# Attention's values as two products of reduced-width parts, with the weights scaled on ScalarE

## The chip, the cores and the metric

The kernel runs on one core of one Trainium2 chip. The metric is the device time of one execution in microseconds (us), the median of several runs. Engines are called PE (TensorE; PEld is its weight load), DVE (VectorE), ACT (ScalarE), POOL (GpSimd) and SP (SyncE, which issues the DMAs).

## What is computed

A two-layer trunk for 1024 prompt tokens and 64 sample tokens. Each layer projects the normalised input once, feeds three branches (a gated linear recurrence, a sparse attention, a state-space scan), and projects their concatenation back. The change touches the end of the attention branch:

```python
logits = jnp.einsum('bqgrd,bqkgd->bqgrk', qg, ksel) * (ATT_HEAD_DIM ** -0.5)
logits = jnp.where(valid, logits + bias, -jnp.inf)
p = jax.nn.softmax(logits, axis=-1)
o = jnp.einsum('bqgrk,bqkgd->bqgrd', p, vsel)
y_b = o * jax.nn.silu(ga)
```

There are 8 query heads in 2 groups (`g`) of 4, head size 64. The kernel keeps all keys and masks those that are not selected.

## The kernel before

Products with full precision are mostly made of float32r parts: a matrix is split into a high part (a float32r copy) and a low part (the rest), and the products of the parts are summed in PSUM. `three` (L210) does this for the projections: L215, L216 and L217 are its three products. Attention's logits (L1068) use two parts. The values (L1098) do not: they multiply plain float32 operands.

Attention works on items `(t, g)`: a tile `t` of 128 queries (t = 8 is the 64 sample tokens) and a head group. The list `todo` gives their order: all of g = 0, the wide ones (t = 5, 8, 7, 6) last, then g = 1 as t = 2, 1, 0, 3, 8, 4, 5, 6, 7. A tile t has 128(t+1) keys; t = 8 has 576. For each item

- `queries` loads and splits the queries, and transposes them (L1034);
- `weigh` makes for each of the 4 heads the logits in PSUM (L1068), adds mask and bias and takes the maximum on DVE (L1071), exponentiates on ACT (L1075), and scales the row by the reciprocal of its sum on DVE (L1077, L1078);
- `values` goes over blocks of 128 keys. For each block PE transposes the weights of the 4 heads into one of two `tp` banks (L1093), ACT copies that bank to SBUF as `pT` (L1095), and PE multiplies with the values (L1098), the stationary operand being 64 columns of `vt`, one matmul for each pair of heads, into the two halves of the partitions of the single `s1` bank. At the end DVE multiplies with the gate (L1100) and DMAs store the result.

There are 82 blocks in each layer: 72 with 128 queries, 10 of the sample tile with 64. Two items are in flight: `weigh` of the next item is written ahead of `values` of this one, and the weights live in 8 buffers `lg`.

The order on each engine is not that of the source. A scheduler that simulates the program while it is built places each instruction by priority, as soon as its own model of the engines has it ready. So attention, which comes first in the source, is interleaved on PE with the first half of the output projection that follows it (`out_proj(0, ...)`: 576 products of L215 to L217). These products are called the filler here: they depend on the other branches only, and PE takes them where the scheduler saw attention waiting.

The values `vt` come from three DMAs at the start of attention (L980 to L982), beside the loads of the keys (L986 to L989), which pass through two of the `lg` buffers.

Of the kernel before, what the change touches and what calls it, by code (L numbers as in the profile page):

```python
# [10 lines left out]
F32 = mybir.dt.float32  # L11
F32R = mybir.dt.float32r
# [25 lines left out]
TS = 64  # L38
# [44 lines left out]
def body(ctx, tc, I, O):  # L83
# [36 lines left out]
    def s1_bank():  # L120
        return bank("s1", 1)
# [157 lines left out]
    for l in range(DEPTH):  # L279
# [684 lines left out]
                    done(d, ci, a, b, ps)  # L964

        kst = kp.tile([128, 2, 2, TP + PAST + TS], F32R, name="kst")
        vt = kp.tile([128, 13, 128], F32, name="vt")
        def near_bias(g):

            nb = kp.tile([128, 4, 256], F32, name="nb")  # L970
# [6 lines left out]

        nb = near_bias(0)

        SP.dma_start(vt[:, 0:8, :], kvd[:, 0:8, 128:256])  # L980
        SP.dma_start(vt[:, 8:12, :], I["cache_att_v"][l])
        SP.dma_start(vt[:TS, 12, :], kvd[:TS, 8, 128:256])  # L982
        kf, kc_ = [p.tile([128, 1024], F32, name="lg", bufs=8) for _ in range(2)]
        kf = kf.rearrange("p (t c) -> p t c", c=128)
        SP.dma_start(kf, kvd[:, 0:8, 0:128])
# [52 lines left out]
        def weigh(t, g, qst):  # L1038

            nq = rows_of(t)  # L1040
            kbase, nk, near, nb0 = reach(t)
            far = nk - near
            mk = mask[t - 2] if t >= 2 else None

            parts = [(c, min(c + 512, far), False) for c in range(0, far, 512)]
            if parts and parts[-1][1] - parts[-1][0] + near <= 512:
                banks = [[x] for x in parts[:-1]] + [[parts[-1], (far, nk, True)]]
            else:
                banks = [[x] for x in parts] + [[(far, nk, True)]]
            mx = p.tile([128, 4, 4], F32, name="mx")  # L1050
            sm = p.tile([128, 4], F32, name="sm")
            ri = p.tile([128, 4], F32, name="ri")
            lgs = []
            for h in range(4):
                lg = p.tile([128, 1024], F32, name="lg", bufs=8)
                lgs.append(lg)
                k_ = 0
                if mk is not None:
                    nbm = p.tile([128, 256], F32, name="nbm")
                    G.tensor_tensor(nbm[:nq, :near], nb[:nq, h, nb0:nb0 + near], mk[:nq, far:nk], op=OP.add)  # L1060
                    nbm = nbm[:nq, :near]
                else:
                    nbm = nb[:nq, h, nb0:nb0 + near]
                for bank_ in banks:
                    a, b = bank_[0][0], bank_[-1][1]
                    ps = s2_bank()
                    for pt in range(2):
                        PE.matmul(ps[:nq, :b - a], qst[:, h, :nq], kst[:, g, pt, kbase + a:kbase + b],  # L1068
                                  start=pt == 0, stop=pt == 1)
                    for f, e, varies in bank_:  # L1070
                        V.tensor_tensor_reduce(lg[:nq, f:e], ps[:nq, f - a:e - a], nbm if varies else mk[:nq, f:e], 1.0,  # L1071
                                               3.0e38 if k_ == 0 else mx[:nq, h, k_ - 1:k_], OP.add, OP.min,
                                               mx[:nq, h, k_:k_ + 1])
                        k_ += 1
                S.activation(lg[:nq, :nk], lg[:nq, :nk], AF.Exp, scale=-1.0, bias=mx[:nq, h, k_ - 1:k_],  # L1075
                             accum_out=sm[:nq, h:h + 1])
                V.reciprocal(ri[:nq, h:h + 1], sm[:nq, h:h + 1])  # L1077
                V.tensor_scalar(lg[:nq, :nk], lg[:nq, :nk], ri[:nq, h:h + 1], None, op0=OP.mult)  # L1078
            return lgs

        def values(t, g, lgs):

            nq = rows_of(t)
            nk = reach(t)[1]
            ga = p.tile([128, 2, 128], F32, name="ga", bufs=1)
            SP.dma_start(ga[:, :, :nq], gad[:, 2 * g:2 * g + 2, t * 128:t * 128 + nq])
            av = s1_bank()[:, :256].rearrange("p (r q) -> p r q", r=2)
            nb_ = (nk + 127) // 128
            for j in range(nb_):
                n = min(128, nk - 128 * j)  # L1090
                ps = tp_bank()
                for i, h in enumerate((0, 2, 1, 3)):
                    PE.transpose(ps[:n, i * nq:(i + 1) * nq], lgs[h][:nq, j * 128:j * 128 + n], ident[:nq, :nq])  # L1093
                pT = p.tile([128, 4, 128], F32, name="pT")
                S.activation(pT[:n, :, :nq], ps[:n, :4 * nq].rearrange("p (r q) -> p r q", r=4), AF.Copy)  # L1095
                vj = j + (8 if t == 8 else 0)
                for b in range(2):
                    PE.matmul(av[64 * b:64 * b + 64, :, :nq], vt[:n, vj, 64 * g:64 * g + 64], pT[:n, 2 * b:2 * b + 2, :nq],  # L1098
                              start=j == 0, stop=j == nb_ - 1)
            V.scalar_tensor_tensor(ga[:, :, :nq], av[:, :, :nq], 0.5, ga[:, :, :nq], op0=OP.mult, op1=OP.mult)  # L1100
            for i in range(2):
                SP.dma_start(ybd[2 * g + i][:, t * 128:t * 128 + nq], ga[:, i, :nq])

# [130 lines left out]
```

## Time and profile before

| what | value |
|---|---|
| median of 3 runs | 2048.23 us (2042.67 to 2052.76) |
| the profiled execution's own time | 2043.88 us |
| its span | 2042.1 us |
| PE busy | 1952.6 us (96%) |
| DVE busy | 1519.2 us (74%) |
| ACT busy | 1231.8 us (60%) |
| POOL busy | 651.2 us (32%) |
| mean granted TensorE clock | 0.983 |

The span reaches from the first to the last instruction; the own time lies 1.8 us above it. The two layers do the same work, and attention stands once in each: in the first from about 700 to 948 us of the span, in the second from about 1709 to 1955 us. Busy shares over the whole span mix stages with different limits; the rows further down are cut by stage.

### The profile page before, as it was taken

What the parts mean: (1) busy time and instruction counts of PE and PEld (TensorE: products, weight loads), DVE (VectorE), ACT (ScalarE), POOL (GpSimd) and SP (SyncE); (2) the same over time, 40 slices, a digit from 0 to 9 for tenths busy, and PEclk for the clock granted to TensorE, in tenths of its full rate; (3) what the DMA queues carried; (4) which work ended last, traced back from release to release, by engine and by line L of the source; (5) the groups of instructions that cost most, each with busy time, mean ns of one, the idle gap of its engine ahead of it and who ended that gap; (6) DMA issues with size and microseconds to landing.
All of it is one profiled execution on the core that took longest, in us unless ns stands there. A gap on an engine that the chain in (4) does not pass through costs nothing.

```text
span 2042.1 us, 34620 instructions
## 1 busy us (share of the span) xinstructions
PE 1952.6 (96%) x12056; PEld 1747.9 (86%) x12056; DVE 1519.2 (74%) x3701; ACT 1231.8 (60%) x2567; POOL 651.2 (32%) x561
## 2 busy tenths in 40 slices
PE   6999999989999899999999999999899999999999
PEld 5899989888889787866998999999888887888589
DVE  7778899898866855574386888999987678566723
ACT  6569988753656544454355798987446655444621
POOL 3012244333522422253430213353245224223320
PEclk9999999999999899999999999999999998999999
DMA  6125354535332732324541343545353346234145
GB/s 228 62 72 143 101 167 123 173 105 154 107 109 83 231 116 89 106 89 137 191 134 38 108 124 108 161 137 165 99 163 97 96 149 197 90 99 140 46 145 169
DMA packets 252079, 257.94 MB, mean 126 GB/s; under 512 B 31264, under 2 KB 230304, under 8 KB 251904
## 3 DMA queue, kind: packets, MB, share of 16 engines
q1 hardware_dynamic: 251904, 255.73, 40.9%
q8 instruction: 95, 1.56, 0.3%
q14 instruction: 80, 0.66, 0.1%
HBM read 181.09 MB, written 74.57 MB: 125 GB/s over the span
## 4 chain that ended last, share of the span: by engine, by line
PE 66%; DVE 19%; DMA 6%; ACT 5%; issue 3%; SPq 1%; POOL 0%; DVEq 0%; ACTq 0%
PE mm L216 16%; PE mm L215 15%; PE mm L217 15%; PE s L1098 4%; PE tp L1093 4%; PE s L1068 3%; DVE u L855 2%; ACT junka L580 2%; PE s L881 1%; DMA cumB<-cumd 1%; PE s L514 1%; DMA eB<-cumd 1%; ACT cumB L742 1%; DMA xsc<-xsd 1%; PE s L791 1%
## 5 line engine op out<-in xcount | busy, mean ns | idle before, releaser
L193 POOL TENSOR_TENSOR wlo<-wraw,whi 128x1024 fp32r<-128x1024 f32 x80 | 195.4, 2442 | 364.0 <-ACT whi L192 360.3
L580 ACT ACTIVATE junka<-sc,cand 128x768 bf16<-128x768 f32 x248 | 239.4, 968 | 8.5 <-DVE sc L583 3.9
L192 ACT ACTIVATE whi<-wraw 128x1024 fp32r<-128x1024 f32 x130 | 137.1, 1054 | 135.3 <-PE mm L216 109.8
L1075 ACT ACTIVATE lg<-lg,mx 128x512 f32<-128x512 f32 (+8 forms) x144 | 111.2, 773 | 95.7 <-DVE mx L1071 95.3
L855 DVE SCALAR_TENSOR_TENSOR u<-raw,parh,u 128x384 f32<-128x384 f32 (+1 forms) x198 | 147.4, 751 | 11.7 <-POOL u L853 5.9
L1095 ACT ACTIVATE pT<-tp 128x512 f32<-128x512 f32 (+1 forms) x164 | 90.5, 568 | 108.1 <-PE tp L1093 103.5
L1060 POOL TENSOR_TENSOR nbm<-nb,shared 128x256 f32<-128x256 f32 (+1 forms) x112 | 81.2, 730 | 224.1 <-DVE mx L1071 201.8
L574 DVE TENSOR_SCALAR_CACHE_REDUCE junk<-sc,cand 128x384 bf16<-128x384 f32 (+4 forms) x194 | 139.9, 753 | 1.0
L1068 PE MATMUL s<-kst,qst 128*128 128x512 f32 (+4 forms) x448 | 120.8, 362 | 7.8 <-DVE mx L1071 7.3
L742 ACT ACTIVATE cumB<-cumB,ctk 128x128 f32<-128x128 f32 (+1 forms) x288 | 88.4, 384 | 54.3 <-DMA cumB<-cumd 47.7
L1093 PEld LDWEIGHTS tp<-identr,lg 128*128 128x128 f32 (+2 forms) x656 | 71.8, 140 | 45.6 <-issue 39.4
L1093 PE MATMUL tp<-identr,lg 128*128 128x128 f32 (+2 forms) x656 | 107.2, 278 | 0.5 <-DVE lg L1078 0.5
L1098 PE MATMUL s<-pT,vt 128*64 128x256 f32 (+2 forms) x656 | 104.8, 389 | 1.6 <-ACT pT L1095 1.6
L1078 DVE TENSOR_SCALAR lg<-lg,ri 128x512 f32<-128x512 f32 (+8 forms) x144 | 93.6, 651 | 3.3
L1143 DVE TENSOR_TENSOR xl<-xl,mm 128x384 f32<-128x384 f32 (+1 forms) x40 | 21.4, 540 | 94.1 <-PE mm L217 84.9
L1068 PEld LDWEIGHTS s<-kst,qst 128*128 128x128 f32 (+1 forms) x448 | 72.2, 188 | 21.9 <-DVE mx L1071 13.4
L215 PE MATMUL mm<-sth0a,whi 128*128 128x384 f32 (+1 forms) x228 | 82.9, 365 | 7.3 <-DVE xl L1143 2.0
L1071 DVE CUSTOM_DVE_ANT_0 lg<-s,shared 128x512 f32<-128x512 f32 (+4 forms) x112 | 61.8, 553 | 37.7 <-PE s L1068 31.9
L193 DVE TENSOR_TENSOR wlo<-wraw,whi 128x1024 fp32r<-128x1024 f32 x50 | 64.1, 1281 | 32.1 <-ACT whi L192 32.0
L216 PE MATMUL mm<-stl1a,whi 128*128 128x384 f32 (+1 forms) x228 | 79.6, 349 | 3.8 <-DVE stl1a L954 3.5
L216 PE MATMUL mm<-stl0a,whi 128*128 128x384 f32 (+1 forms) x228 | 79.8, 350 | 2.4 <-POOL stl0a L954 2.0
L778 POOL TENSOR_TENSOR hT<-hT,dec 128x512 f32<-128x512 f32 x28 | 35.9, 1282 | 144.3 <-DVE hT L780 137.0
(475 smaller groups left out, 6931.1 us busy)
## 6 DMA issues: line engine op xcount, KB each, us to landing
wraw<-in_w_in_dram SPq DMA_DIRECT2D x82, 512.0 KB, 3.5
wraw<-in_w_out_dram SPq DMA_DIRECT2D x48, 512.0 KB, 3.8
cumB<-cumd SPq DMA_DIRECT2D x32, 512.0 KB, 4.8
xsd<-u SPq DMA_DIRECT2D x48, 192.0 KB, 2.4
gz<-gzd SPq DMA_DIRECT2D x32, 256.0 KB, 3.6
xsc<-xsd SPq DMA_DIRECT2D x32, 256.0 KB, 3.5
eB<-cumd SPq DMA_DIRECT2D x56, 128.0 KB, 4.1
gzd<-g SPq DMA_DIRECT2D x32, 192.0 KB, 1.9
```

What stands on the lines that cost most here:

```text
L192: S.activation(hi, raw, AF.Copy)
L193: eng.tensor_tensor(lo, raw, hi.bitcast(F32), op=OP.subtract)
L215: PE.matmul(ps, hi[:, k, :], xh[ci][:, c0:], start=k == 0, stop=False)
L216: PE.matmul(ps, hi[:, k, :], xl[ci][:, c0:], start=False, stop=False)
L217: PE.matmul(ps, lo[:, k, :], xh[ci][:, c0:], start=False, stop=k == len(xs) - 1)
L574: V.tensor_scalar(junk, sc[j][:n], thr, None, op0=op, op1=OP.add, accum_out=out)
L580: S.activation(junk, sc[j][:n], AF.Sign, scale=-1.0, bias=cand, accum_out=out)
L855: V.scalar_tensor_tensor(u, raw[:, j:j + n], w[:, wbase + j * wstride:wbase + j * wstride + 1], u, op0=OP.mult, op1=OP.add)
L1068: PE.matmul(ps[:nq, :b - a], qst[:, h, :nq], kst[:, g, pt, kbase + a:kbase + b], start=pt == 0, stop=pt == 1)
L1075: S.activation(lg[:nq, :nk], lg[:nq, :nk], AF.Exp, scale=-1.0, bias=mx[:nq, h, k_ - 1:k_], accum_out=sm[:nq, h:h + 1])
L1093: PE.transpose(ps[:n, i * nq:(i + 1) * nq], lgs[h][:nq, j * 128:j * 128 + n], ident[:nq, :nq])
L1098: PE.matmul(av[64 * b:64 * b + 64, :, :nq], vt[:n, vj, 64 * g:64 * g + 64], pT[:n, 2 * b:2 * b + 2, :nq], start=j == 0, stop=j == nb_ - 1)
```

## The change

The values become float32r parts. `vhl` holds for each block of 128 keys and each group 128 columns: the high part of the 64 value columns beside their low part. The values are loaded into two `lg` buffers first; ACT makes the high part and POOL the low part. In `values`, ACT's copy of the transposed weights becomes the float32r high part `pT`; a new subtraction on DVE makes the low part `pl` from the PSUM bank and `pT`. Two matmuls over all four heads (512 columns) take the place of two float32 ones over two heads each (256 columns); the stationary operand is 128 columns wide, so the products with the high and with the low part of the values land in different partitions. At the end of an item ACT copies two quarters of the `s1` bank into `sm2`, shifted by 64 partitions, DVE adds the other two quarters, and the gate is multiplied from SBUF. In `weigh` the scaling by the reciprocal moves from DVE to ACT.

```diff
-        vt = kp.tile([128, 13, 128], F32, name="vt")
+        vhl = kp.tile([128, 13, 2, 128], F32R, name="vhl")
...
-        SP.dma_start(vt[:, 0:8, :], kvd[:, 0:8, 128:256])
-        SP.dma_start(vt[:, 8:12, :], I["cache_att_v"][l])
-        SP.dma_start(vt[:TS, 12, :], kvd[:TS, 8, 128:256])
+        v0, v1 = [p.tile([128, 1024], F32, name="lg", bufs=8) for _ in range(2)]
+        v0, v1 = [v.rearrange("p (t c) -> p t c", c=128) for v in (v0, v1)]
+        SP.dma_start(v0, kvd[:, 0:8, 128:256])
+        SP.dma_start(v1[:, 0:4, :], I["cache_att_v"][l])
+        SP.dma_start(v1[:TS, 4, :], kvd[:TS, 8, 128:256])
+        for v, n, a, b, c in ((v0, 128, 0, 8, 0), (v1, 128, 8, 12, 0), (v1, TS, 12, 13, 4)):
+            v = v[:n, c:c + b - a].rearrange("p t (g c) -> p t g c", g=2)
+            S.activation(vhl[:n, a:b, :, 0:64], v, AF.Copy)
+            G.tensor_tensor(vhl[:n, a:b, :, 64:128], v, vhl[:n, a:b, :, 0:64].bitcast(F32), op=OP.subtract)
...
-                V.tensor_scalar(lg[:nq, :nk], lg[:nq, :nk], ri[:nq, h:h + 1], None, op0=OP.mult)
+                S.activation(lg[:nq, :nk], lg[:nq, :nk], AF.Copy, scale=ri[:nq, h:h + 1])
...
-            av = s1_bank()[:, :256].rearrange("p (r q) -> p r q", r=2)
+            av = s1_bank().rearrange("p (r q) -> p r q", r=4)
...
-                pT = p.tile([128, 4, 128], F32, name="pT")
-                S.activation(pT[:n, :, :nq], ps[:n, :4 * nq].rearrange("p (r q) -> p r q", r=4), AF.Copy)
+                ps = ps[:n, :4 * nq].rearrange("p (r q) -> p r q", r=4)
+                pT = p.tile([128, 4, 128], F32R, name="pT")
+                pl = p.tile([128, 4, 128], F32R, name="pl")
+                S.activation(pT[:n, :, :nq], ps, AF.Copy)
+                V.tensor_tensor(pl[:n, :, :nq], ps, pT[:n, :, :nq].bitcast(F32), op=OP.subtract)
                 vj = j + (8 if t == 8 else 0)
-                for b in range(2):
-                    PE.matmul(av[64 * b:64 * b + 64, :, :nq], vt[:n, vj, 64 * g:64 * g + 64], pT[:n, 2 * b:2 * b + 2, :nq],
-                              start=j == 0, stop=j == nb_ - 1)
-            V.scalar_tensor_tensor(ga[:, :, :nq], av[:, :, :nq], 0.5, ga[:, :, :nq], op0=OP.mult, op1=OP.mult)
+                for k_, w in enumerate((pT, pl)):
+                    PE.matmul(av[:, :, :nq], vhl[:n, vj, g, :], w[:n, :, :nq], start=j == 0 and k_ == 0,
+                              stop=j == nb_ - 1 and k_ == 1)
+
+            sm2 = p.tile([128, 2, 128], F32, name="sm2", bufs=1)
+            S.activation(sm2[0:64, :, :nq], av[64:128, 0:2, :nq], AF.Copy)
+            S.activation(sm2[64:128, :, :nq], av[0:64, 2:4, :nq], AF.Copy)
+            for b in range(2):
+                c = slice(64 * b, 64 * b + 64)
+                V.tensor_tensor(sm2[c, :, :nq], sm2[c, :, :nq], av[c, 2 * b:2 * b + 2, :nq], op=OP.add)
+            V.scalar_tensor_tensor(ga[:, :, :nq], sm2[:, :, :nq], 0.5, ga[:, :, :nq], op0=OP.mult, op1=OP.mult)
```

The scheduler makes another order of it. In the changed file 6 lines stand above L1028 of before, so L1068 is now L1074, L1075 is L1081 and L1093 is L1099; the scaling is L1084, the copy to `pT` L1103, the subtraction L1104, the values' matmul L1107, the shifted copies L1111 and L1112.

PE, first layer, at the narrow items (2, 1), (1, 1) and (0, 1), early in the second head group. Before (`s_8808` is the result of item (2, 1), L1098 its values):

```order
L1098 MATMUL s_8808<-pT,vt 64x256 x2
L1034 MATMUL tp<-identr,qhl_8841 128x128 x4
L215 MATMUL mm<-sth6b,whi 128x320
L216 MATMUL mm<-stl6b,whi 128x320
L217 MATMUL mm<-sth6b,wlo 128x320
L215 MATMUL mm<-sth7b,whi 128x320
L216 MATMUL mm<-stl7b,whi 128x320
L217 MATMUL mm<-sth7b,wlo 128x320
L215 MATMUL mm<-sth0a,whi 128x384
L216 MATMUL mm<-stl0a,whi 128x384
```

The same place with the change (`s_8943` is the result of item (2, 1), `s_9034` of (1, 1)):

```order
L1107 MATMUL s_8943<-pT,vhl 128x512
L1107 MATMUL s_8943<-pl,vhl 128x512
L1099 MATMUL tp<-identr,lg 128x128 x8
L1074 MATMUL s_9083<-kst,qst 128x512 x2
L1074 MATMUL s_9094<-kst,qst 128x512 x2
L1074 MATMUL s_9105<-kst,qst 128x512 x2
L1074 MATMUL s_9116<-kst,qst 128x512 x2
L1107 MATMUL s_9034<-pT,vhl 128x512
L1107 MATMUL s_9034<-pl,vhl 128x512
L1107 MATMUL s_9034<-pT,vhl 128x512
```

The filler (L215 to L217) that stood between attention's products is gone from here; it has moved ahead, among the wide items of g = 0.

ACT, first layer, in the wide items at the end of g = 1, before (`lg` are weights, L1095 the copies of transposed blocks):

```order
L1095 ACTIVATE pT<-tp 128x512
L1075 ACTIVATE lg,sm<-lg,mx 128x896
L1075 ACTIVATE lg,sm<-lg,mx 128x1024
L1095 ACTIVATE pT<-tp 128x512 x2
L1075 ACTIVATE lg,sm<-lg,mx 128x1024
L953 ACTIVATE sth7a<-g_10657 128x384
L1095 ACTIVATE pT<-tp 128x512
L1075 ACTIVATE lg,sm<-lg,mx 128x1024
```

The same place with the change:

```order
L1103 ACTIVATE pT<-tp 128x512 x2
L1081 ACTIVATE lg,sm<-lg,mx 128x1024
L1111 ACTIVATE sm_9690<-s_9623 64x256
L1112 ACTIVATE sm_9690<-s_9623 64x256
L1103 ACTIVATE pT<-tp 128x512
L1084 ACTIVATE lg<-lg,ri 128x1024
L1081 ACTIVATE lg,sm<-lg,mx 128x1024
L1103 ACTIVATE pT<-tp 128x512 x2
L1081 ACTIVATE lg,sm<-lg,mx 128x1024
L1084 ACTIVATE lg<-lg,ri 128x1024 x2
```

Each exponential has got a scaling of its own width in the same queue, and each item two shifted copies; the copies that release PE's `tp` banks stand among them.

## Rows read from the trace of the kernel before

**Rows 1.** The page: its busy line and the engines of the chain that ended last.

```profile
PE 1952.6 (96%) x12056; PEld 1747.9 (86%) x12056; DVE 1519.2 (74%) x3701; ACT 1231.8 (60%) x2567; POOL 651.2 (32%) x561
...
PE 66%; DVE 19%; DMA 6%; ACT 5%; issue 3%; SPq 1%; POOL 0%; DVEq 0%; ACTq 0%
```

**Rows 2.** Windows, first layer's attention, cut where items (1,0), (6,0), (0,1), (8,1), (7,1) end.

```profile
core 0: us, PE busy (x) PEld busy (x) DVE busy (x) ACT busy (x) POOL busy (x), PEclk, DMA share, GB/s
707.29:845.12 137.83, 137.83 (x868) 110.84 (x867) 75.24 (x252) 62.24 (x126) 34.73 (x37) 1.00 0.34 104
845.12:868.09 22.97, 22.97 (x150) 18.97 (x151) 15.38 (x57) 12.51 (x33) 7.23 (x7) 1.00 0.46 139
868.09:901.86 33.77, 32.87 (x207) 25.54 (x205) 24.27 (x67) 17.20 (x40) 20.17 (x20) 1.00 0.39 120
901.86:947.71 45.85, 42.81 (x264) 23.87 (x262) 29.41 (x98) 29.92 (x55) 12.49 (x13) 1.00 0.17 51
```

**Rows 3.** Timeline of PE at three places: start us, us, engine, line, operation.

```profile
713.33 0.63 PE L1068 MATMUL s<-kst,qst 128*128 128x512 f32 x2
713.80 0.33 PE L215 MATMUL mm<-sth4a,whi 128*128 128x384 f32 x1
713.97 0.34 PE L216 MATMUL mm<-stl4a,whi 128*128 128x384 f32 x1
...
717.17 0.71 PE L1068 MATMUL s<-kst,qst 128*128 128x512 f32 x2
717.72 0.27 PE L1093 MATMUL tp<-identr,lg 128*128 128x128 f32 x1
...
909.05 0.66 PE L1093 MATMUL tp<-identr,lg 128*128 128x128 f32 x4
909.47 0.37 PE L1068 MATMUL s<-kst,qst 128*128 128x256 f32 x1
...
941.52 0.65 PE L1098 MATMUL s<-pT,vt 128*64 128x256 f32 x4
942.10 0.66 PE L1093 MATMUL tp<-identr,lg 128*128 128x128 f32 x4
942.69 0.65 PE L1098 MATMUL s<-pT,vt 128*64 128x256 f32 x4
```

**Rows 4.** Groups of ACT by form, 901.86 to 947.71 us.

```profile
L1095 ACT ACTIVATE pT<-tp 128x512 f32<-128x512 f32 x26 | 15.0, 593 | 10.2 <-PE tp L1093 9.5 <-PE s L1098 0.4 <-ACT lg L1075 0.2
L1075 ACT ACTIVATE lg<-lg,mx 128x1024 f32<-128x1024 f32 x4 | 4.6, 1147 | 2.3 <-DVE mx L1071 2.3
L1075 ACT ACTIVATE lg<-lg,mx 128x896 f32<-128x896 f32 x4 | 4.2, 1038 | 1.1 <-DVE mx L1071 1.1
L1075 ACT ACTIVATE lg<-lg,mx 128x768 f32<-128x768 f32 x4 | 3.8, 938 | 1.6 <-DVE mx L1071 1.6
L1075 ACT ACTIVATION_READ_ACCUMULATOR lg<-lg,mx 128x1 f32 x13 | 2.5, 190 | 0.0
```

**Rows 5.** Timeline of ACT: how instructions in a row overlap.

```profile
904.78 1.09 ACT L1095 ACTIVATE pT<-tp 128x512 f32<-128x512 f32 x2 [0.16 <-ACT lg L1075]
905.75 0.94 ACT L1075 ACTIVATE lg<-lg,mx 128x768 f32<-128x768 f32 x1
```

**Rows 6.** Groups of DVE by form, 680 to 948 us.

```profile
L1107 DVE TENSOR_TENSOR g<-g,mm 128x384 f32<-128x384 f32 x16 | 8.8, 550 | 11.1 <-PE mm L217 10.8
...
L1078 DVE TENSOR_SCALAR lg<-lg,ri 128x896 f32<-128x896 f32 x8 | 5.6, 705 | 0.1
```

**Rows 7.** Windows of 5 us ahead of attention, and one in its last items.

```profile
670.00:675.00 5.00, 2.70 (x22) 2.44 (x20) 3.05 (x7) 2.62 (x5) 1.86 (x1) 1.00 0.70 229
675.00:680.00 5.00, 2.97 (x10) 1.92 (x9) 5.00 (x10) 1.30 (x3) 3.27 (x3) 0.55 0.92 283
...
925.00:930.00 5.00, 3.96 (x20) 2.18 (x22) 4.94 (x18) 4.15 (x8) 3.14 (x3) 1.00 0.39 111
```

**Rows 8.** Timeline of PE: the transposes of the keys, ahead of attention.

```profile
674.41 0.87 PE L999 MATMUL tp<-identr,pT 128*128 128x128 f32 x8 [2.30 <-ACT kst L1005]
```

## The prediction

> **What bounds the kernel now.** I read the page first: PE is busy 96% of the span and carries 66% of the chain that ended last, DVE 19%, ACT 5% [rows 1]. So PE is the bound on average; whether it is in attention is read there. The windows cut the first layer's attention at the ends of items [rows 2]: the wide items of g = 0 take 137.8 us, the narrow ones of g = 1, (2,1), (1,1), (0,1), take 23.0, then (3,1) and (8,1) 33.8, and the last four wide ones 45.9, together 240.4 us. PE is busy in 236.5 of these. The reader is to see two things in the rows. PE has no idle time in the first two stretches, because filler stands in them (by the order of PE's queue 423 products and 68; then 93, and 6 in the last). And in the last stretch, where filler has run out, PE still leads with 42.8 of 45.9 us, against 29.9 on ACT and 29.4 on DVE. A change that takes work from PE pays here as long as ACT and DVE stay behind it.
>
> **TensorE's part.** A block of the values costs PE the transposes of four heads and the float32 product. In the last item blocks follow each other with nothing between: 941.52 to 942.69, 1.17 us [rows 3]. With the change the product is two float32r matmuls of 512 columns. L1068 has that form: a pair takes 0.47 us behind filler (713.33 to 713.80) and 0.55 behind a transpose (717.17 to 717.72). Four transposes ahead of such a pair take 0.42 (909.05 to 909.47) [rows 3]. So a block costs 0.42 + 0.47 to 0.42 + 0.55, 0.89 to 0.97 us, and saves 0.20 to 0.28. I take 0.21, since most pairs stand behind transposes, and 0.10 for the blocks of the sample tile, which are half as wide. With 72 and 10 of them that is 16 us in a layer and 32 in all, if PE sets the time.
>
> A rule speaks against this saving: the Trainium skill (FP8 and Floating Point Precision, TensorE Precision Notes) says that a true FP32 product makes four passes through the array. By an estimate from that page, four passes of 256 columns for two halves of the array side by side are as many columns as two passes of 512, and nothing would be saved. The rows disagree: the float32 product alone takes 0.58 us (941.52 to 942.10), the float32r pair 0.47 to 0.55 [rows 3].
>
> **ScalarE's and VectorE's part.** ACT gets a scaling beside each exponential. The trace before has no scaling on ACT from SBUF at these widths; the exponentials of the same tiles are the nearest rows: 1147, 1038 and 938 ns at 1024, 896 and 768 columns [rows 4]. I take these as they are. It also gets two shifted copies of 64x256 an item, between zero and the 593 ns of a 512-column copy [rows 4]; by the slope of the exponentials (209 ns for 256 columns) some 0.38 us. DVE loses its scalings (705 ns at 896 columns) and gets a subtraction of 128x512 out of PSUM for each block. The nearest row subtracts nothing but reads PSUM and SBUF alike, 550 ns at 384 columns [rows 6]; in proportion 0.73, at one column each 1.04 ns more 0.68. I take 0.68. Per item it also gets two adds of some 0.4 us.
>
> **Stretch by stretch, one layer.** The scheduler has moved filler: by the new order of PE 523, 1, 48 and 6 products stand in the four stretches. A filler product costs 0.17 us at 384 columns (713.80 to 713.97) [rows 3]; a third have 320, so 0.165.
>
> First: 137.8 + 100 x 0.165 - 34 x 0.21 - 5 x 0.10 = 146.7 us. ACT (62 of 138 us before) and DVE (75) have room here; each stays under 100.
>
> Second: PE falls to 23.0 - 67 x 0.165 - 6 x 0.21 = 10.7 us. ACT and DVE keep 12.5 and 15.4 [rows 2] and add scalings, exponentials that now stand here, subtractions, copies and adds: by their order and the prices above 18 to 22 us each. They set the end now. I take 22, against 23.0 before.
>
> Third: 33.8 - 45 x 0.165 - 4 x 0.21 - 5 x 0.10 = 25.0 us; ACT and DVE come to 18 to 23. I take 25.
>
> Fourth: PE alone would need 45.9 - 26 x 0.21 = 40.4. ACT's queue holds 26 copies (15.4 us), 12 exponentials (12.5), 12 scalings (12.5), their reads (2.3), 8 shifted copies (3.1) and three others (1.6): 47.4 us. Instructions in a row overlap by about 0.1 us (two copies and the next exponential start 0.97 apart, and the copies last 1.09) [rows 5]; for 75 of them that takes 7.5 off, so 40 us bare. At the 93% that PE reached before (42.8 of 45.9) it is 43. The last item's 8 blocks then cannot go faster than a bank's round (transpose 0.6, copy 0.6, subtraction 0.7, for two banks 1.0 us a block), some 4 us more than their copies alone, and its two copies and two adds at the end 1.5. Together 48.
>
> Sum: 146.7 + 22 + 25 + 48 = 241.7 against 240.4, 1.3 us more in a layer, 2.6 in both. The split of the values ahead of attention I cost at nothing: 2 us on ACT and a few on POOL lie in front of the keys' evacuation, for which PE waits 2.3 us already [rows 8], but the three loads now go out earlier, and the small load of keys stood behind them. If that cover is gone it costs up to 4 us a layer. The profiled execution took 2043.9 us, 4.3 below the median of 2048.2. On the median's level the sum is 2048.2 + 2.6, rounded to **2051 us**.
>
> **The rivals.** *TensorE's saving comes through.* ACT and DVE lag nowhere, the filler only changes places, and the time falls by up to 32 us, to 2016. For it: over a whole layer's attention ACT's and DVE's work stays under 170 us of 240, and the scheduler put exponentials well ahead. Against it: in the second and fourth stretch the order leaves PE nothing to do while ACT and DVE work 18 us and 40. It decides if those stretches take under 19 and 43 us.
>
> *The clock falls in the stretches without filler.* This ends on the other side. Ahead of attention PE was busy 2.70 of 5 us, and in the next 5 the granted clock was 0.55, that is mostly 1.2 GHz instead of 2.4; at 3.96 of 5 us in the last items it stayed at 1.00 [rows 7]. With the change the second stretch has 10.7 us of PE work in 22. At 1.2 GHz that work doubles and joins the chain copy, subtraction, transpose: I put 5 us there, 4 in the filler behind it until the clock is back, and 6 in the fourth stretch if it falls there too (33 of 48 us busy): 15 a layer, 30 in all, 2080. It decides if the granted clock of the second stretch falls clearly below 1.00; the rows have work like that of either kind. The Trainium skill (TensorE: Matmul & The Clock Gate, Part 1) says the same in kind, that the slow clock is the default and activity releases it; the rows ahead of attention agree with it.
>
> *The split of the values holds up the keys.* 4 to 6 us a layer in front of attention, where the clock is low already: 2060.
>
> *No saving on TensorE.* If the float32r block takes its old 1.17 us, the first stretch takes 7.6 us more, and the others hardly change, as ACT sets them: 2066.
>
> **How the numbers follow.** Forecast 0.41, TensorE's saving 0.29, clock 0.19, keys 0.07, no saving 0.04. About 0.5% (10 us) is what a measurement of this kernel can tell from no change: faster is under 2038, slower over 2058.5. The forecast's own range is 2034 to 2062, most of it inside (0.34, with 0.04 faster and 0.03 slower). The faster rival gives 0.28 to faster and 0.01 to same, the clock 0.18 to slower and 0.01 to same, the keys 0.05 and 0.02, the last 0.04 to slower: 0.32, 0.38 and 0.30. With all bounds low (144, 18, 22 and 41 us) a layer takes 225, 15 less, so 2018; with all high (148, 28, 28, 54, and 4 ahead) 262, so 2092. The range leaves about one in ten out on either side: 2022 to 2084.
>
> **What would show it.** In the profile after: L1098's float32 rows give way to pairs at 0.47 to 0.55 us; the same windows read about 147, 22, 25 and 48 us; in the second PE's busy share is near half, and in the fourth ACT is busier than PE; the copy to `pT` waits for PE less than before, and PE's weight load for `pl` or `pT` more. The forecast is wrong if PE is still busy nine tenths in the fourth stretch (then the first rival), if the granted clock in the second and third lies well under 1.00 (the second), or if the first stretch is as long as before.

## The result and the profile after

The change takes 2076.09 us (median of 4 runs, 2075.08 to 2081.94), the kernel before beside it 2047.9 (4 runs). The ratio is 1.0129, with a 95% interval of 1.0107 to 1.0150: slower by 28 us. The profiled executions lie further apart, 2081.94 against 2043.88 us, so of the 38 us between the two traces some 10 belong to the executions and not to the change.

The page of the changed kernel, its busy line and the engines of the chain that ended last:

```profile
PE 1947.4 (94%) x11728; PEld 1781.5 (86%) x11728; DVE 1558.6 (75%) x3793; ACT 1354.3 (65%) x2789; POOL 655.6 (32%) x567
...
PE 56%; DVE 20%; ACT 9%; DMA 8%; issue 4%; SPq 1%; POOL 0%; DVEq 0%; ACTq 0%; POOLq 0%
```

Against [rows 1] PE has lost 10 points of the chain, most of them to ACT and DMA, and ACT is busy 122 us longer. The windows answer to [rows 2], cut at the ends of the same items. First the four stretches of the first layer, then the second and third of the second layer:

```profile
717.54:862.38 144.84, 141.80 (x876) 131.44 (x874) 89.62 (x276) 95.11 (x182) 44.11 (x44) 1.00 0.37 115
862.38:887.41 25.03, 18.21 (x80) 12.30 (x80) 17.73 (x71) 20.61 (x55) 6.25 (x9) 0.79 0.23 65
887.41:918.45 31.04, 28.61 (x135) 22.94 (x135) 18.17 (x57) 19.58 (x41) 9.93 (x11) 0.79 0.24 70
918.45:966.59 48.14, 39.29 (x193) 26.32 (x193) 36.30 (x107) 40.52 (x70) 8.76 (x10) 1.00 0.21 60
...
1893.45:1913.91 20.46, 16.55 (x77) 10.53 (x77) 16.40 (x66) 18.24 (x49) 5.29 (x8) 0.92 0.37 102
1913.91:1942.97 29.06, 26.22 (x137) 21.72 (x137) 18.77 (x60) 20.38 (x43) 10.23 (x12) 0.88 0.25 75
```

The four take 249.1 us in the first layer (240.4 before) and 242.8 in the second (239.1 before). The second and third stretch of the second layer before:

```profile
1853.11:1875.18 22.07, 22.07 (x144) 18.15 (x144) 14.82 (x57) 12.75 (x33) 8.27 (x9) 1.00 0.49 146
1875.18:1908.31 33.13, 30.67 (x201) 24.60 (x199) 24.76 (x63) 16.27 (x38) 17.45 (x18) 1.00 0.39 117
```

Two columns say what is new. PE was busy all the time in the second stretch; now it is idle for 6.8 of 25.0 us. And the granted clock, 1.00 in all of these stretches before, is 0.79 in the first layer and 0.92 in the second there, and 0.79 and 0.88 in the third stretch.

What PE waits for in the second stretch, PE's timeline:

```profile
862.53 0.49 PE L1107 MATMUL s<-pT,vhl 128*128 128x512 f32 x1 [2.15 <-ACT pT L1103]
863.58 0.79 PE L1107 MATMUL s<-pl,vhl 128*128 128x512 f32 x1 [0.55 <-DVE pl L1104]
...
884.35 0.38 PE L1099 MATMUL tp<-identr,lg 128*128 128x128 f32 x2
888.38 0.80 PE L1107 MATMUL s<-pT,vhl 128*128 128x512 f32 x1 [3.65 <-ACT pT L1103]
```

No filler stands between these rows: PE transposes at 884.35, and the copy that it needs next comes from ACT at 887.75. ACT's timeline shows what ACT did in between:

```profile
884.10 0.38 ACT L1111 ACTIVATE sm<-s 64x256 f32<-64x256 f32 x1
884.49 0.38 ACT L1112 ACTIVATE sm<-s 64x256 f32<-64x256 f32 x1
884.89 0.77 ACT L1081 ACTIVATE lg<-lg,mx 64x576 f32<-64x576 f32 x1
885.57 0.19 ACT L1081 ACTIVATION_READ_ACCUMULATOR lg<-lg,mx 64x1 f32 x1
885.66 0.76 ACT L1084 ACTIVATE lg<-lg,ri 64x576 f32<-64x576 f32 x1
886.33 0.76 ACT L1081 ACTIVATE lg<-lg,mx 64x576 f32<-64x576 f32 x1
...
887.75 1.05 ACT L1103 ACTIVATE pT<-tp 128x512 fp32r<-128x512 f32 x2
```

The shifted copies, exponentials and scalings stand in one queue ahead of the copy, and PE has nothing else to run.

One sum will carry the comparison. A window's length is PE's work at full speed (busy time by granted clock), plus PE's idle time, plus what a low clock costs (busy time by one less the clock). Summed over the lead-in (from the first copy of transposed keys to the end of the first item) and the four stretches of the first layer, in us (the clock is read to two digits, so the terms are good to about 1 us):

| kernel | length | work | idle | low clock |
|---|---|---|---|---|
| before | 274.0 | 257.6 | 9.3 | 7.1 |
| the change | 288.1 | 244.2 | 28.7 | 15.2 |

The lead-in's own windows, before and then the change:

```profile
673.76:707.29 33.53, 28.21 (x146) 23.57 (x147) 30.47 (x88) 20.27 (x55) 20.78 (x20) 0.75 0.73 227
```

```profile
678.45:717.54 39.09, 31.48 (x181) 27.73 (x182) 35.70 (x95) 28.48 (x74) 27.19 (x25) 0.83 0.64 200
```

In the second layer the length goes from 276.9 to 280.9, with work 255.8 and 246.0, idle time 12.9 and 25.2, low clock 8.2 and 9.7. So TensorE's saving is there, 13.4 and 9.7 us a layer (lead-in and stretches hold 648 filler products in both kernels, and 654 in the second layer before). Idle time, 19.4 and 12.3 us more, and the low clock, 8.1 and 1.5 more, took more than that back.

### The profile page after: what moved, and what is told of

Read it like the earlier page. It is cut to its first block, busy times and chain, and to the rows that moved or that the text cites. A ratio compares the mean times of both kernels' runs of the same rounds, so it can differ in the third digit from the quotient of the medians.

```text
span 2080.0 us, 34234 instructions
## 1 busy us (share of the span) xinstructions
PE 1947.4 (94%) x11728; PEld 1781.5 (86%) x11728; DVE 1558.6 (75%) x3793; ACT 1354.3 (65%) x2789; POOL 655.6 (32%) x567
## 4 chain that ended last, share of the span: by engine, by line
PE 56%; DVE 20%; ACT 9%; DMA 8%; issue 4%; SPq 1%; POOL 0%; DVEq 0%; ACTq 0%; POOLq 0%
PE mm L216 14%; PE mm L215 14%; PE mm L217 14%; PE s L1074 2%; PE s L1107 2%; PE tp L1099 2%; ACT junka L580 2%; DMA cumB<-cumd 2%; DVE u L855 2%; ACT cumB L742 1%; PE s L881 1%; PE s L514 1%; ACT lg L1081 1%; DMA eB<-cumd 1%; ACT lg L1084 1%
## 5 line engine op out<-in xcount | busy, mean ns | idle before, releaser
L1066 POOL TENSOR_TENSOR nbm<-nb,shared 128x256 f32<-128x256 f32 (+1 forms) x112 | 76.5, 685 | 248.1 <-DVE mx L1077 215.7
L1081 ACT ACTIVATE lg<-lg,mx 128x512 f32<-128x512 f32 (+8 forms) x144 | 110.9, 771 | 44.4 <-DVE mx L1077 43.8
L1104 DVE TENSOR_TENSOR pl<-tp,pT 128x512 fp32r<-128x512 f32 (+1 forms) x164 | 106.1, 654 | 30.2 <-ACT pT L1103 29.6
L1074 PE MATMUL s<-kst,qst 128*128 128x512 f32 (+4 forms) x448 | 120.1, 360 | 8.1 <-DVE mx L1077 7.4
L1103 ACT ACTIVATE pT<-tp 128x512 fp32r<-128x512 f32 (+1 forms) x164 | 90.9, 563 | 49.9 <-PE tp L1099 46.3
L1084 ACT ACTIVATE lg<-lg,ri 128x512 f32<-128x512 f32 (+8 forms) x144 | 109.4, 769 | 14.5 <-DVE ri L1083 14.1
L1099 PE MATMUL tp<-identr,lg 128*128 128x128 f32 (+2 forms) x656 | 102.8, 273 | 2.2 <-DVE pl L1104 1.1
L1099 PEld LDWEIGHTS tp<-identr,lg 128*128 128x128 f32 (+2 forms) x656 | 79.7, 142 | 20.1 <-issue 2.0
L215 PE MATMUL mm<-sth0a,whi 128*128 128x384 f32 (+1 forms) x228 | 84.3, 372 | 10.0 <-DVE xl L1159 5.6
L1074 PEld LDWEIGHTS s<-kst,qst 128*128 128x128 f32 (+1 forms) x448 | 71.7, 187 | 21.0 <-DVE mx L1077 11.9
L1077 DVE CUSTOM_DVE_ANT_0 lg<-s,shared 128x512 f32<-128x512 f32 (+4 forms) x112 | 61.7, 552 | 33.4 <-PE s L1074 19.4
L1107 PE MATMUL s<-pT,vhl 128*128 128x512 f32 (+1 forms) x164 | 69.0, 421 | 13.6 <-ACT pT L1103 8.2
## 6 DMA issues: line engine op xcount, KB each, us to landing
gz<-gzd SPq DMA_DIRECT2D x32, 256.0 KB, 3.6
xsc<-xsd SPq DMA_DIRECT2D x32, 256.0 KB, 3.5
```

Source lines behind the costliest of these rows:

```text
L215: PE.matmul(ps, hi[:, k, :], xh[ci][:, c0:], start=k == 0, stop=False)
L1084: S.activation(lg[:nq, :nk], lg[:nq, :nk], AF.Copy, scale=ri[:nq, h:h + 1])
```

## The experiments

All were timed beside the kernel before on the same chip, four versions to a chip; the times stand as ratios to it, with their 95% intervals. The kernel before took 2053.25, 2054.48 and 2052.33 us there, and the expectations name times on the level of 2048, so a ratio times 2048 is what compares with them. Two theories came from the traces: (A) the scalings in ACT's queue, (B) the loads and the split of the values ahead of attention, where the first item ends 10.3 us later in the trace (717.54 against 707.29 us).

**The scaling back on VectorE.**

```diff
-                S.activation(lg[:nq, :nk], lg[:nq, :nk], AF.Copy, scale=ri[:nq, h:h + 1])
+                V.tensor_scalar(lg[:nq, :nk], lg[:nq, :nk], ri[:nq, h:h + 1], None, op0=OP.mult)
```

> The change with the scaling of the weights put back on VectorE, nothing else. Two theories. (A) The loss lies in attention's queue on ScalarE: the scalings there delay the copies to pT, the scheduler then spends the filler early, and the narrow items of the second group run without it. Then this run gives back most of the loss inside attention: the second, third and fourth stretch fall from 25, 31 and 48 us to about 21, 29 and 44, some 10 us a layer, and the time to about 2056 us. (B) The loss lies ahead of attention, in the loads and the split of the values: the first item still ends as late as with the change, and the time stays within 5 us of 2076.

Measured: 1.0144 (1.0118 to 1.0169), as slow as the change. Theory A's figures are missed: the fourth stretch took 49.5 us in both layers, not 44. The third fell, to 27.2 and 27.5 us at a clock of 1.00, but the second ran at 0.67 and 0.76.

**Only the scaling on ScalarE**, in the kernel before, the same two lines exchanged.

> The kernel before with only the scaling moved to ScalarE; values stay float32. Theory A (ScalarE's queue): filler moves ahead and the stretches two and four get longer as with the change, by 2 to 5 us a layer; about 2055 us. Theory B (lead-in): no more than 5 us from 2048 in either direction.

Measured: 0.9977 (0.9961 to 0.9993), some 5 us faster than before. So the scaling on ACT is no cost to the kernel before; by itself it is at most a small gain, 1 to 8 us by the interval. Where it lies its trace doesn't show: lead-in and stretches are 2.2 and 3.7 us longer there than before. This is the one version here below both kernels that leaves nothing out.

**The split written later**: the block from `v0, v1 = ...` to the subtraction moved behind `all_keys(0)`.

```diff
         all_keys(0)
+        v0, v1 = [p.tile([128, 1024], F32, name="lg", bufs=8) for _ in range(2)]
...
```

> The change with the loads and the split of the values written behind the keys of the first group. Theory B (lead-in): 5 to 7 us a layer come back in front of attention, the wait of TensorE before the keys' transposes falls from 3.7 to about 2.3 us, VectorE's subtractions for the cached keys fall from 1.75 to 1.89 back to about 0.68 us since GpSimd no longer subtracts beside them; about 2064 us. Theory A: the first item ends earlier, but the time stays within 5 us of 2076, as the filler that was run meanwhile is missing later.

Measured: 1.0113 (1.0088 to 1.0138), not told apart from the change. One expectation failed for a plain reason: the scheduler left the subtractions on GpSimd where they were (the first 2.1 us behind the first copy of transposed keys, 2.0 with the change), so VectorE's subtractions still took 1.46 and 1.75 us. So this run hardly tests theory B; the next one does.

**The split alone**: the kernel before, with the block of the change added and its results unused.

```diff
+        vhl = kp.tile([128, 13, 2, 128], F32R, name="vhl")
...
+        v0, v1 = [p.tile([128, 1024], F32, name="lg", bufs=8) for _ in range(2)]
...
```

> The kernel before with the loads of the values into two lg buffers and their split added, the parts not being used (the products stay float32, with the values loaded as before, so 0.8 MB are loaded twice in a layer). Theory B (lead-in): 5 to 7 us a layer more in front of attention, about 2060 us. Theory A: within 5 us of 2048.

Measured: 1.0000 (0.9981 to 1.0020). Theory B falls: by itself the split costs nothing that can be told (4 us either way). What made the lead-in look longer was filler. Windows of the lead-in, before and then the change, of L215 alone (us, PE busy and count, PEld, clock, DMA):

```profile
673.76:707.29 33.53, 8.82 (x20) 4.91 (x21) 0.75 0.73 227
```

```profile
678.45:717.54 39.09, 11.16 (x31) 6.30 (x31) 0.83 0.64 200
```

It has 11 more of L215, and 31 more products of the three lines; at 0.165 us that is 5.1 of the 5.6 us. They are missing later, and cost nothing by themselves. With the split alone the lead-in has 58 of them (60 before, 91 with the change) and takes 34.0 us.

Scaling and split together don't explain the loss, so it lies in the products of parts and in what they do to the order. Two further theories: (F) filler is gone from the narrow items; (L) the chain of a block is too long.

**Filler held back.** A tiny copy on VectorE into the first column of `wraw` makes the load of the last two weight blocks of the first half wait for the last item of g = 0.

```diff
+HOLD = {6: 0, 7: 0}
+MARK = {8: 0}
...
+        if held is not None:
+            V.tensor_copy(raw[:, 0:1], held)
...
+            if i in MARK:
+                V.tensor_copy(held[:, MARK[i]:MARK[i] + 1], last_ga[0][:, 0, 0:1])
```

> The change with a quarter of the filler held back: the weights of the seventh and eighth block of the first half of the output projection are loaded only when the last item of g = 0 has its result, so some 60 products stand in the second stretch again and 140 in the third, and 362 in the first. Two theories for the loss that neither the scaling nor the split explains by itself. (F) The filler is gone from the narrow items, TensorE idles there and its clock falls. Then the second and third stretch run at a granted clock of 1.00, the first falls by some 20 us to about 125, the second stays at 23 to 25, the third is some 38, the fourth 48: about 235 us for a layer where 249 and 243 were, and the time is about 2055 us. (L) The chain of a block (copy, subtraction, two products, a bank that comes free late) is too long for TensorE to be kept busy, with or without filler. Then the idle time only moves into the first stretch, where 362 products are left, and the time stays within 6 us of 2076.

Measured: 1.0085 (1.0062 to 1.0109), 2071.51 us. Windows of its four stretches, first layer:

```profile
714.03:837.61 123.58, 117.52 (x714) 104.53 (x713) 80.23 (x261) 87.97 (x172) 27.82 (x33) 1.00 0.29 88
837.61:864.86 27.25, 25.78 (x148) 22.74 (x149) 19.34 (x65) 21.74 (x53) 7.90 (x8) 0.94 0.50 148
864.86:901.81 36.95, 36.68 (x218) 32.22 (x217) 28.32 (x78) 23.83 (x51) 23.88 (x23) 1.00 0.49 153
901.81:955.37 53.56, 43.45 (x208) 29.46 (x206) 37.24 (x110) 41.20 (x71) 9.46 (x11) 0.97 0.18 54
```

Theory F holds for the middle: idle time in stretches two and three falls from 9.2 to 1.7 us, and the clock is back to 0.94 and 1.00. It doesn't hold for the whole: idle time moves to the first stretch (6.1 us, 3.0 with the change), and the fourth grows to 53.6. About a third of the 28 us comes back, though the interval still touches that of the change. Both theories named a number, 2055 and 2076; by the ratio it is 2065 on the level of 2048, half way between.

**Filler held in three steps**, `HOLD = {5: 0, 6: 1, 7: 2}` and `MARK = {4: 0, 7: 1, 10: 2}`.

> The same with three holds: the sixth block of weights waits for the fifth item, the seventh for the eighth item, the eighth for the eleventh, so filler stands in all four stretches (about 388, 46, 91 and 53 products). Theory F: TensorE idles less than with one hold, the clock stays at 1.00, about 2045 us. Theory L: within 6 us of 2076.

Measured: 1.0101 (1.0073 to 1.0130). No better than one hold: idle time stands in all four stretches (4.8, 5.5, 0.8 and 8.6 us in the first layer).

**Three banks for transposes**, two for the projections.

```diff
-        return bank("mm", 3)
+        return bank("mm", 2)
...
-        return bank("tp", 2)
+        return bank("tp", 3)
```

> The change with three PSUM banks for transposes instead of two, and two instead of three for the projections. Theory L: the bank's round is no longer the limit, the fourth stretch falls from 48 to about 44 us, the second and third by 2 to 4, unless the projections outside attention lose by the missing bank; about 2060 us. Theory F: within 6 us of 2076 unless the scheduler leaves filler in the second stretch, which by the new order it does (75 and 87 products); then as in the run with held filler.

Measured: 1.0167 (1.0136 to 1.0198). Outside attention it loses, as the expectation allowed: up to the keys it takes 688.8 us (678.4 with the change), and from the last item of the first layer to the keys of the second 758.6 (744.0). Inside, its first two stretches read

```profile
729.80:856.67 126.87, 126.87 (x792) 117.54 (x792) 82.01 (x261) 89.30 (x171) 31.46 (x32) 0.99 0.36 110
856.67:879.86 23.19, 23.19 (x149) 21.59 (x147) 16.10 (x60) 18.26 (x44) 7.22 (x8) 1.00 0.47 140
```

PE has no idle time in these two, and the four stretches come to 228.9 and 234.1 us a layer, against 249.1 and 242.8. The fourth moves less (47.5 and 45.9, theory L had 44). But part of this has moved into the lead-in, where PE is idle for 12.5 and 15.2 us (7.6 with the change), and 24 and 11 filler products have left the windows: lead-in and stretches together are 269.9 us against 288.1 in the first layer, and 279.3 against 280.9 in the second.

**Without the low part of the weights** (it leaves out `pl` and its product).

```diff
-                V.tensor_tensor(pl[:n, :, :nq], ps, pT[:n, :, :nq].bitcast(F32), op=OP.subtract)
...
-                for k_, w in enumerate((pT, pl)):
+                for k_, w in enumerate((pT,)):
```

> The change without the low part of the weights: no subtraction for pl and one product a block, so the weights enter the values with their float32r part alone. It prices the low part. By TensorE's time alone 82 products of 0.235 us in a layer, 19 us, so 38 in all and about 2038 us, if the idle time stays as it is (theory F alone). Theory L: the chain is shorter by the subtraction too, and the stretches with idle time fall further: 2025 us or less.

Measured: 0.9888 (0.9862 to 0.9914), 2032.06 us. Its four stretches in the first layer:

```profile
716.28:840.93 124.65, 124.65 (x795) 117.80 (x795) 62.87 (x230) 90.85 (x177) 38.04 (x38) 1.00 0.42 125
840.93:863.50 22.57, 19.40 (x113) 15.20 (x112) 19.14 (x69) 20.78 (x53) 12.94 (x14) 0.89 0.45 131
863.50:890.48 26.98, 23.70 (x135) 20.73 (x133) 15.36 (x51) 20.48 (x45) 9.72 (x12) 0.90 0.27 81
890.48:936.83 46.35, 34.15 (x170) 23.68 (x170) 21.64 (x85) 41.34 (x71) 9.45 (x11) 0.93 0.21 62
```

By the number this is theory L's: the ratio makes it 2025 us on the level of 2048, 49 less than the change, where TensorE's time alone was to give 38. By the mechanism it is not. Without the subtraction PE's idle time in lead-in and stretches is 26.8 and 29.1 us a layer, about what it is with it (28.7 and 25.2). What fell is PE's work, by 24.1 and 22.3 us a layer, 0.29 and 0.27 for each of the 82 products and not 0.235. The fourth stretch is 46.4 us although DVE is busy for only 21.6 of it; ACT is busy for 41.3.

**A third bank that only attention gets.** To keep the projections' three banks, one bank is the projections' third outside attention and the transposes' third inside it. In the change, in the kernel before, in the kernel before with the scaling on ACT, and in the change with the late split:

```diff
+        return bank("mx", 1) if shared and turn[tag] % 3 == 0 else bank(tag, 2)
...
-                ps = tp_bank()
+                ps = tp_bank(True)
```

> The change with a third PSUM bank for the transposed weights, taken from the projections' three only while attention runs: every third transpose tile of the values goes to a bank of its own, which outside attention and in the second half of the output projection is the projections' third. Theory L (the round of two banks: transposes, copy, subtraction, transposes again): the first stretch falls to about 128 us and attention to some 230 to 236 us a layer, as with three transpose banks everywhere, the scheduler keeps filler in the second stretch (92 and 85 products by its order), and without that run's losses outside attention the time is about 2050 us. Theory F alone (only where the filler stands matters): the same gain as from holding filler, about 2070 us.

Measured: 1.0188 (1.0160 to 1.0216).

> The kernel before with the same third bank. Theory L says that the float32 kernel hardly waits for a bank, since its round has no subtraction: within 5 us of the kernel before. If it gains as much as the change does (20 us or more), the bank is a gain of its own and says nothing on the change.

Measured: 1.0114 (1.0087 to 1.0141).

> The kernel before with the scaling on ScalarE and the third bank, the float32 products kept. If scaling and bank add up, some 5 us below the kernel before; if the run of the bank in the changed kernel comes out lower than this, the products of parts pay once the bank is there.

Measured: 1.0101 (1.0075 to 1.0126).

> The change with the third bank and with the loads and the split of the values written behind the keys of the first group. The late split alone measured within its error of the change; with the bank the keys may set the lead-in again, so 0 to 6 us less than the change with the bank alone. The candidate for beating both kernels, at 2045 us or so.

Measured: 1.0145 (1.0118 to 1.0171). All four miss. The sharing itself costs time outside attention: the kernel before with it needs 687.8 us up to the keys and 744.4 between the layers' attention, 14 us more each than without. Inside attention it decides little: in the changed kernel the first stretch falls to 132.7 and 134.6 us, without idle time, but the second grows to 32.0 and 30.9, and the four stretches take 243.2 and 244.5 us, 234.1 and 236.5 with the late split as well, 242.6 and 248.9 in the kernel before (240.4 and 239.1 without). So how much of the change's loss the two banks make was not settled.

The sum of lead-in and four stretches for the runs that decide, length = work + idle + low clock, first layer and second:

| kernel | first layer | second layer |
|---|---|---|
| only scaling on ACT | 276.1 = 256.0 + 11.5 + 8.6 | 280.7 = 259.3 + 14.5 + 6.8 |
| only the split | 274.0 = 253.4 + 14.2 + 6.4 | 275.0 = 255.2 + 13.2 + 6.6 |
| scaling on DVE | 288.4 = 245.0 + 27.7 + 15.7 | 287.9 = 243.5 + 29.5 + 14.9 |
| filler held | 280.4 = 246.5 + 25.7 + 8.2 | 278.8 = 245.9 + 24.6 + 8.3 |
| no low part | 259.0 = 220.1 + 26.8 + 12.1 | 266.2 = 223.8 + 29.1 + 13.3 |

The kernels with float32 products have 11.5 to 14.5 us idle in these rows, those with products of parts 24.6 to 29.5.

The traces also say what PE's idle time stands in front of. In the four stretches, PE's idle time in all and the part of it that is a wait ahead of the values' transposes and products, in us, first layer and second (what ended a wait is inferred from semaphores):

| kernel | idle time | ahead of the values |
|---|---|---|
| before | 3.9, 5.5 | 1.0, 1.0 |
| only scaling on ACT | 5.4, 6.2 | 2.4, 2.5 |
| only the split | 5.8, 5.3 | 1.5, 1.0 |
| the change | 21.1, 17.6 | 12.6, 7.9 |
| scaling on DVE | 19.9, 20.4 | 9.4, 11.1 |
| no low part | 18.7, 19.6 | 6.9, 6.2 |
| three banks for transposes | 10.5, 14.1 | 4.3, 5.3 |

So most of what the change adds, 11.6 of 17.2 us and 6.9 of 12.1, is waiting in the block's chain: for the copy to `pT` (6.8 and 1.5), for the subtraction (3.7 and 2.3), in the second layer also for the scalings (2.5). Theory L holds to this extent: the waits get shorter without the subtraction and with a third bank. Without the subtraction others take their place, mostly ahead of filler products (4.2 and 6.5 us, 2.4 and 3.2 with the change).

## Why the prediction was right and wrong

The point, 2051 us, was 25 us too low; the range of 2022 to 2084 holds 2076. Step by step:

**TensorE's price was right for products in a row.** Four products in a row, PE's timeline of the changed kernel:

```profile
943.63 0.47 PE L1107 MATMUL s<-pT,vhl 128*128 128x512 f32 x1
943.94 0.40 PE L1107 MATMUL s<-pl,vhl 128*128 128x512 f32 x1
944.17 0.40 PE L1107 MATMUL s<-pT,vhl 128*128 128x512 f32 x1
944.40 0.40 PE L1107 MATMUL s<-pl,vhl 128*128 128x512 f32 x1
944.64 0.60 PE L1099 MATMUL tp<-identr,lg 128*128 128x128 f32 x4
```

The first two start 0.31 us apart, the others 0.23: a pair takes 0.47 to 0.54, where 0.47 to 0.55 was read from [rows 3]. Four transposes take 0.36 us ahead of such a product (957.65 to 958.01, below), less than the 0.42 that was read; ahead of the float32 product they had taken 0.59 (942.10 to 942.69) [rows 3]. So most of a block's saving lies in the transposes, little in the product. The saving of 16 us a layer came as 13.4 and 9.7 of PE's work; the products don't always stand in a row: one with `pl` took 0.33 us ahead of transposes (959.67 to 960.00, below), and 0.27 to 0.29 on the mean by the run without the low part. The rival without a saving falls. The Trainium skill (FP8 and Floating Point Precision, TensorE Precision Notes) gives a true FP32 product four passes through the array, and by the estimate worked out from that it would have cost as much as the pair; it took 0.58 us, a difference of 0.04 to 0.11, and the measurement decides.

**ScalarE's and VectorE's prices were right.** Groups by form in the fourth stretch, ACT and then DVE:

```profile
L1084 ACT ACTIVATE lg<-lg,ri 128x1024 f32<-128x1024 f32 x4 | 4.5, 1138 | 0.0
L1084 ACT ACTIVATE lg<-lg,ri 128x896 f32<-128x896 f32 x4 | 4.2, 1040 | 0.0
L1111 ACT ACTIVATE sm<-s 64x256 f32<-64x256 f32 x4 | 1.5, 381 | 1.4 <-PE s L1107 1.3
```

```profile
L1104 DVE TENSOR_TENSOR pl<-tp,pT 128x512 fp32r<-128x512 f32 x26 | 17.7, 688 | 6.3 <-ACT pT L1103 6.3
```

Forecast were 1147, 1038, 380 and 680 ns. ACT's work in that stretch is 40.5 us against "40 us bare".

**First and fourth stretch: right.** 144.8 in both layers against 146.7, and 48.1 and 48.5 against 48. ACT is the busier engine in the fourth, as said. One detail was short: the last item's blocks go at 1.18 us on the mean, not 1.0. A bank's round, on PE, ACT and DVE:

```profile
957.65 0.60 PE L1099 MATMUL tp<-identr,lg 128*128 128x128 f32 x4
958.01 0.47 PE L1107 MATMUL s<-pT,vhl 128*128 128x512 f32 x1
...
959.67 0.50 PE L1107 MATMUL s<-pl,vhl 128*128 128x512 f32 x1
960.00 0.60 PE L1099 MATMUL tp<-identr,lg 128*128 128x128 f32 x4
```

```profile
958.29 0.60 ACT L1103 ACTIVATE pT<-tp 128x512 fp32r<-128x512 f32 x1 [0.53 <-PE tp L1099]
```

```profile
958.92 0.69 DVE L1104 TENSOR_TENSOR pl<-tp,pT 128x512 fp32r<-128x512 f32 x1 [0.44 <-ACT pT L1103]
```

Transposes, copy and subtraction end at 959.61, but the next transposes into that bank stand behind the product with `pl` in PE's queue and start at 960.00: 2.35 us for two banks. The working had left that product out. The float32 kernel needed 1.17 a block [rows 3], so at the end of attention the change gains nothing.

**Second stretch: length nearly right, clock not.** 25.0 and 20.5 us against 22. PE idles as foreseen; the forecast had put the price of the clock at nothing.

**The step that failed is the third stretch, "I take 25".** It took 31.0 and 29.1 us. The sum took PE's remaining work there at full speed; without what the low clock costs, the two are 25.0 and 25.9. Windows of 10 us where the second stretch gives way to the third:

```profile
870.00:880.00 10.00, 7.77 (x30) 5.04 (x29) 8.28 (x32) 7.99 (x20) 2.99 (x5) 0.67 0.15 42
880.00:890.00 10.00, 5.63 (x26) 3.40 (x25) 6.93 (x26) 9.94 (x22) 2.38 (x4) 0.84 0.20 53
890.00:900.00 10.00, 9.07 (x28) 7.45 (x27) 4.85 (x13) 3.37 (x8) 4.75 (x5) 0.50 0.58 172
```

After the idle time the granted clock is 0.50 from 890 to 900 us, 1.2 GHz, while PE has work and is busy for 9.07 of 10 us. Over the second and third stretch the low clock costs 3.8 + 6.0 us in the first layer (18.21 x 0.21 and 28.61 x 0.21) and 1.3 + 3.1 in the second. This is the rival of the clock, by the condition that it named. Its price was 15 us a layer: 9.8 and 4.4 came, its 6 in the fourth stretch did not (1.00). The rule cited there, that the slow clock is the default and activity releases it (the Trainium skill, TensorE: Matmul & The Clock Gate, Part 1), agrees in kind: with filler held back for these stretches the clock read 0.94 and 1.00.

This step makes 10 of the 25 us that the point was short, 6.0 in one layer and 4.1 in the other. The second and fourth stretch add 2 together, the first takes off 4. The lead-ins, put at nothing, took 5.8 us more in the two traces, and the rest lies outside the sum's windows.

**The split at nothing: right.** 1.0000 by itself. The longer lead-in was filler that the new order had put there, which the sum, made from the four stretches, had not counted.

**The first rival** (the saving comes through) fell at its own points: the second stretch is not under 19, the fourth not under 43.

**What stays open.** In the traces 12.3 us of the difference lie in the eight stretches and 5.8 in the two lead-ins. The other 19.7 lie outside: 4.7 ahead of the first keys, 13.3 between the two layers' attention, 1.7 behind the last item. Much of that is not the price of products of parts: the trace of the split alone, a kernel as fast as before, is 7.4 us longer than the trace before ahead of the first keys and 8.7 between the layers' attention. Executions differ in their clock, too. From 10 to 60 us of the span, 600 us ahead of the values' loads, the windows read 1.00 before, then the change, then the split alone:

```profile
10.00:60.00 50.00, 42.27 (x239) 37.45 (x240) 43.96 (x140) 31.21 (x67) 15.44 (x15) 1.00 0.59 199
```

```profile
10.00:60.00 50.00, 42.03 (x214) 36.77 (x215) 41.86 (x132) 29.72 (x64) 15.04 (x15) 0.93 0.61 201
```

```profile
10.00:60.00 50.00, 43.02 (x201) 37.86 (x202) 39.86 (x122) 28.62 (x63) 14.97 (x15) 0.86 0.57 190
```

The last of them is the lowest, in a kernel that isn't slower than before. Some 10 of the 38 us between the two traces are the distance of these executions from their medians; where these 10 lie isn't shown, and the source of the rest outside attention was not found. Nor is it settled why idle time doubles with products of parts. Shown is that it stays when the scaling goes back to VectorE and when the subtraction for `pl` is left out, that the split alone doesn't bring it, and that most of it stands ahead of the values' transposes and products. No run tested the end of an item alone, two shifted copies and two adds before the single `s1` bank is free again, which all versions with products of parts share; PE's waits for these adds are 1.3 and 1.6 us a layer. And every version has its own order from the scheduler, so no run changes the chain and nothing else. That ACT's and DVE's work sets the length of the late stretches, so that work taken from PE there turns into idle time, is argued from the fourth stretch, which took between 44.6 and 54.2 us in every run.

## What to carry to other kernels

A saving on the busiest engine pays only where that engine sets the time. Here two others stood just behind it, the saving turned into idle time, and with the idle time the clock of the work that followed fell. Filler is part of this: the scheduler spent it earlier, so count where it stands before and after, lead-in included. And price a part by adding it alone: the scaling and the split looked guilty in the trace, and cost nothing that could be measured when run by themselves.

## What was not expected of the hardware

VectorE's subtraction for the cached keys, 128x512 with both inputs in SBUF, took 0.68 us before. Timeline of DVE, before and then with the change, and of POOL with the change:

```profile
675.65 0.68 DVE L1012 TENSOR_TENSOR kst<-lg,kst 128x512 fp32r<-128x512 f32 x1
```

```profile
682.98 3.56 DVE L1018 TENSOR_TENSOR kst<-lg,kst 128x512 fp32r<-128x512 f32 x2
```

```profile
680.45 4.58 POOL L988 TENSOR_TENSOR vhl<-lg,vhl 128x1024 fp32r<-128x1024 f32 x3
```

Beside GpSimd's subtractions two of them took 3.56 us, 1.78 each. The Trainium skill (SBUF — State Buffer, Who interferes with whom) says that a VectorE instruction with two inputs in SBUF contends with a GpSimd instruction that reads SBUF, because its second input comes through a read interface that the two share. The rows agree that one holds up the other. Before, VectorE's instruction was the first to start, and GpSimd's subtraction that began 0.16 us behind it took 1.38 us (L954, 128x384), where the same one took 1.01 with the change. PE waited 3.10 us in the lead-in for a later instruction of that queue. It cost nothing in the end: the kernel with the split alone has the same pair at 3.55 us and is as fast as before.
